# Whole-chunk sample attention with the last-landed tile first, and the mixers' weight loads from SP

## The chip, the cores and the metric

The kernel runs on one core of one Trainium2 chip. The metric is the time of one execution on the device in microseconds (us); the kernel before took 1676.75 us (median of 3 runs, 1676.6 to 1680.71).

## What is computed

One inference step of a two-layer decoder trunk in float32, for 256 tokens of a new sequence (the prompt) and 64 tokens that continue eight cached sequences (the sample, 8 each).

```python
D_MODEL = 1024; SEQ = 256; DEC_BATCH = 8; DEC_SEQ = 8; PAST_LEN = 2048; PAGE_SIZE = 128; D_FF = 2816
# each layer:
#   x += 0.5 * SwiGLU(RMSNorm(x))
#   x += W_out [HGRN2 | RWKV-7 | MLA](RMSNorm(x) @ W_in)
#   x += 0.5 * SwiGLU(RMSNorm(x))
# one RMSNorm ends the stack
```

MLA is an attention with a low-rank cache: for each cached token a latent of 256 numbers (ckv) and a rotary key of 32 (kpe). The prompt attends to itself. Each sample token attends to its sequence's 2048 cached tokens, which lie in 16 pages of 128 tokens each, found through a page table, and to the new ones. HGRN2 and RWKV-7 are recurrences, done in chunks.

## The kernel before

Activations are kept transposed, 128 features by 320 tokens to a tile. Each dense weight is loaded as float32 ("raw"), cast on ACT into a high part (L422), and DVE takes the difference as a low part (L423); PE does three matmuls a block of 128 x 128: high x high, high x low and low x high. Weights of the ffn stages come from `wf` in transfers of 512 KB, issued by SP; those of the mixers from `wm` in transfers of 256 KB, issued by ACT (`fetch_raw`, L363), where a load is placed after the cast before last (`issue_after`, which orders instructions for the scheduler). Four raw buffers are used in turn.

The stages follow each other: ffn, mixer 0, ffn, ffn, mixer 1, ffn. A mixer begins with dense work alone: `mla_in` and `mla_q`, which make the queries. Then `weave` (L513) interleaves generators: the input projections, the two recurrences (rw, hg), the prompt's attention (`prompt`), the sample's attention (`sample`) and the part of the output projection that is ready (`w_out`). A generator yields the time at which its next step will be ready in the planner's own count of PE time (`self.pe`), and `weave` takes the first one that is. The order so written is then scheduled by the framework. At the end `mix_out` (L603) does the rest of the output projection.

The sample works on four pairs of sequences p, each in four chunks ch of 512 cached tokens. `scores(p, ch)` needs four ct tiles (keys, 96 x 768, for one sequence and two pages each), `values(p, ch)` four cn tiles (128 x 512). Each tile is loaded by two DMAs, one a page, whose page number SP reads from the table into a register before it; so a chunk of either kind takes eight gathers on SP. There are five buffers for ct tiles and five for cn tiles. For the values the scores are transposed on PE (L290), copied by DVE to PT, and multiplied. The pairs run one behind the other: values of pair p and scores of pair p + 1 alternate.

When a chunk may be planned is set by `ready` (L843): it charges 1.05 us of planned time for each page load, 4 at a time (half a chunk), and lets loads start no earlier than the end of the half-chunk three back. This is where the planner learns that buffers and SP's time are limited:

```python
f[0] = max(f[0], f[1][f[2] - 3] if f[2] > 2 else 0.0) + n * (PACE[1] if f[2] < PACE[0] else 1.05)
```

Of the kernel before, what the change touches and what calls it, by code (L numbers as in the profile page):

```python
# [26 lines left out]
RANK = 256  # L27
# [4 lines left out]
NPOOL = 160  # L32
PAGE = 128
NPAGE = 16
# [2 lines left out]

FBLK, MBLK = 8, 4
LEVELS = [32, 16, 8, 4, 2, 1]
PACE = (0, 1.05)  # L40
ORDER_A = lambda fill, sample: (sample, fill)
ORDER_B = lambda prompt, sample: (sample, prompt)

# [213 lines left out]
class Kern:  # L257
    def __init__(self, ctx, tc, ap):
        self.ctx, self.tc, self.nc, self.ap = ctx, tc, tc.nc, ap
        P = lambda name, bufs, **k: ctx.enter_context(tc.tile_pool(name=name, bufs=bufs, **k))  # L260
        self.cp = P("cp", 1)
        self.xp = P("xp", 1)
        self.wp = P("wp", 1)
        self.ps = P("ps", 1, space=bass.MemoryType.PSUM)
        self.n = 0
        self.gat, self.early, self.casts = [], [], []
        self.pe = 0.0

        self.st = {"wf": [FBLK, 0, None, None], "wm": [MBLK, 0, self.wp, None]}
        self.cur = "wf"  # L270
# [92 lines left out]
    def fetch_raw(self, i):  # L363
        n, _, pool, _ = self.st[self.cur]
        raw = self.t(pool, [128, n * 128], "raw", bufs=RAW)
        if self.cur == "wf":
            return raw, self.nc.sync.dma_start(raw, self.ap["wf"][i])

        with self.tc.issue_after(self.casts[-2]) if len(self.casts) > 1 else ExitStack():
            return raw, self.nc.scalar.dma_start(raw, self.ap["wm"][i])  # L370

    def fetch(self):
        raw, ins = self.fetch_raw(len(self.early))
# [176 lines left out]
    def mixer(self, l):  # L550
        nc, tc = self.nc, self.tc
        self.l = l
        self.pe, self.ready, self.ended, self.ev = 0.0, {}, [], {}
        xh, xl = self.tiles(self.xh, KD), self.tiles(self.xl, KD)
        pool = lambda name: tc.tile_pool(name=f"{name}{l}", bufs=1)
        with pool("mx") as self.mp, pool("ms") as self.sp, tc.tile_pool(name=f"mk{l}", bufs=1, side="right") as self.tb:
            self.idx_setup(l)
            with pool("mq") as self.ta:
                self.mla_in(xh, xl)
                self.mla_q()  # L560
            sample = self.sample()
            with pool("mr") as self.ta:
                rin = self.rw_in(xh, xl)
                for _ in range(17):
                    next(rin)
                rw = [self.together(*[self.chain(self.rw(hp), self.rw_out(hp)) for hp in range(2)])]
                fill, rws = self.chain(rin, self.hg_in(xh, xl), self.outs()), self.rw_split()
                self.urgent = [*rw, rws]
                self.weave([*rw, *ORDER_A(fill, sample), rws], [*rw, fill, rws])
            with pool("mh") as self.ta, pool("mb") as self.tb:  # L570
                hg, prompt, w_out = [self.together(*[self.hg(hp) for hp in range(2)])], self.prompt(), self.w_out()
                self.urgent = [*hg, prompt]
                order = [*hg, *ORDER_B(prompt, sample), w_out]
                self.weave(order, order)

    def outs(self):

# [56 lines left out]
    def mla_in(self, xh, xl):  # L634
        nc, l = self.nc, self.l
        self.mark(f"mla_in{l}")
        cs = self.a([128, T], "cs")
        nc.sync.dma_start(cs, self.ap["cs"])
        self.wukt = self.a([64, NH, 3 * KR], "wukt")
        nc.sync.dma_start(self.wukt.rearrange("p a b -> p (a b)"), self.ap["wukt"][l])  # L640
        self.qh = self.a([128, 3, T], "qh", dt=F32R)
        self.ql = self.a([128, 3, T], "ql", dt=F32R)
        accq = self.a([128, T], "accq")
        acck = self.a([128, T], "acck")
        self.cT = self.m([128, 2, T], "cT")
        first = [self.bank()[:, :T] for _ in range(2)]
        self.dense_pair(first, KD, xh, xl)
        first.append(self.bank("pr")[:, :T])
        self.dense(first[2], KD, xh, xl)
        self.norm_close()  # L650
        for j in range(6):
            if j < 3:
                ps = first[j]
            else:
                ps = self.bank(("pd", "pr")[j % 2])[:, :T]
                self.dense(ps, KD, xh, xl)
            if j == 4:
                pq = self.bank("pa")[:, :T]
                self.mm(pq, self.c("ones"), accq, start=True, stop=True)
                rq = self.rstd_from(pq, self.ta, "rq", 1.0 / 384)  # L660
                self.csq = self.a([128, T], "csq")
                nc.vector.tensor_tensor(out=self.csq, in0=cs, in1=rq, op=ALU.mult)
            if j < 3:
                qa = self.a([128, T], "qa")
                nc.vector.tensor_tensor(out=qa, in0=ps, in1=self.rstd, op=ALU.mult)
                self.sumsq(qa, accq, j == 0)
                self.split_scaled(qa, self.v(l, "gq", j), self.qh[:, j, :], self.ql[:, j, :])
            elif j == 3:
                csr = self.a([128, T], "qa")
                nc.vector.tensor_tensor(out=csr, in0=cs, in1=self.rstd, op=ALU.mult)  # L670

                t1 = self.a([128, T], "rt1")
                nc.vector.tensor_tensor(out=t1[64:], in0=ps[64:], in1=csr[64:], op=ALU.mult)
                for r in (64, 96):
                    nc.vector.tensor_tensor(out=self.kpe[r:r + 32], in0=t1[64:96], in1=t1[96:128], op=ALU.add)
                nc.sync.dma_start(self.ap["o_kpe"][l], self.kpe[64:96, :])
            else:
                nc.vector.tensor_tensor(out=self.cT[:, j - 4, :], in0=ps, in1=self.rstd, op=ALU.mult)
                self.sumsq(self.cT[:, j - 4, :], acck, j == 4)
        self.acck = acck  # L680
# [140 lines left out]
    def sample(self):  # L821
        nc, l = self.nc, self.l
# [12 lines left out]

        def ready(name, n):
            f = feed[name]
            f[0] = max(f[0], f[1][f[2] - 3] if f[2] > 2 else 0.0) + n * (PACE[1] if f[2] < PACE[0] else 1.05)
            f[2] += 1
            return 0, f[0] + 2.2  # L840

# [8 lines left out]

        def scores(p, ch):
            ps = self.bank("pa")
            for hf in range(2):
                yield ready("ct", 4)
                self.mark(f"sample{l}")
                cts = []
                for si in range(2):
                    ct = self.s([KR, 2, 3 * PAGE], "ct", 5)
                    i0 = (2 * p + si) * NPAGE + ch * 4 + hf * 2
                    for pg, r in enumerate(pages(i0, 2)):  # L860
                        self.gat.append(nc.sync.dma_start(ct[:, pg, :], ctp[bass.ds(r + l * NPOOL, 1)].rearrange("a p c -> p (a c)")))
                    cts.append(ct)
                for kt in range(3):
                    for si in range(2):
                        self.mm(ps[64 * si:64 * si + 64, hf * 256:hf * 256 + 256], qlat[:KR, kt, 2 * p + si],
                                cts[si][:, :, kt * PAGE:kt * PAGE + PAGE], start=kt == 0, stop=kt == 2)
                feed["ct"][1].append(self.pe)
            S[p, ch] = self.s([128, 512], "S", 5)
            if ch == 0:
                mx[p] = self.s([128, 8], "smx", 2)  # L870
# [19 lines left out]
            nc.scalar.activation(S[p, ch], S[p, ch], AF.Exp, bias=m[:, 5:6], scale=MLA_SCALE, accum_out=m[:, ch:ch + 1])  # L890

        def values(p, ch, po):
            r0 = ready("cn", 4)
            cns_ = []
            rs = []
            for si in range(2):
                i = (2 * p + si) * NPAGE + ch * 4
                rs.append(pages(i, 4))
            for hf in range(2):
                for si in range(2):  # L900
                    cn = self.s([128, 2, RANK], "cn", 5)
                    for pg in range(2):
                        r = rs[si][hf * 2 + pg]
                        self.gat.append(nc.sync.dma_start(cn[:, pg, :], self.ap["cn"][l, bass.ds(r, 1)].rearrange("a p c -> p (a c)")))
# [8 lines left out]
            PT = self.s([128, 512], "PT", 2)  # L913
            nc.vector.tensor_copy(PT, pt)  # L914
            yield 0, max(self.pe + 1.2, r0[1])
            for hf in range(2):
                self.mark(f"sample{l}")
                for pg in (2 * hf, 2 * hf + 1):
                    for si in range(2):
                        self.mm(po[64 * si:64 * si + 64, :RANK], PT[:, pg * 128 + 64 * si:pg * 128 + 64 * si + 64],  # L920
                                cns_[2 * hf + si][:, pg % 2, :], start=ch == 0 and pg == 0, stop=False)
                feed["cn"][1].append(self.pe)
                if hf == 0:
                    yield ready("cn", 4)

        for ch in range(4):
            yield from scores(0, ch)
# [552 lines left out]
def build(ctx, tc, ap):  # L1480
    K = Kern(ctx, tc, ap)
    for l in range(L + 1):
# [13 lines left out]
            if l < L:  # L1496
                K.ffn(fp, (l, "gm"), False)
        if l < L:
            K.cur, K.casts = "wm", []
            K.mixer(l)  # L1500


# [19 lines left out]
```

## Time and profile before

| | us |
|---|---|
| median of 3 runs | 1676.75 |
| profiled execution | 1678.2 |
| its span | 1676.4 |
| PE busy | 1627.8 (97%) |
| DVE busy | 958.7 (57%) |
| ACT busy | 716.8 (43%) |

The span is the time from the first to the last instruction that the profiler saw. A busy share over the whole span is a mean over stages with different limits: here the ffn stages from 14 to 250, 597 to 1080 and 1426 to 1667 us and the mixers between them. SP does no arithmetic; its time is seen in the starts of the DMA instructions that it issues. "ct<-in_ct x8" is eight gathers that follow each other without another kind between them, with the start of the first and the stretch to the end of the last.

### The profile page before, as it was taken

What the parts mean: (1) busy time and instruction counts of PE and PEld (TensorE: products, weight loads), DVE (VectorE), ACT (ScalarE), POOL (GpSimd) and SP (SyncE); (2) the same over time, 40 slices, a digit from 0 to 9 for tenths busy, and PEclk for the clock granted to TensorE, in tenths of its full rate; (3) what the DMA queues carried; (4) which work ended last, traced back from release to release, by engine and by line L of the source; (5) the groups of instructions that cost most, each with busy time, mean ns of one, the idle gap of its engine ahead of it and who ended that gap; (6) DMA issues with size and microseconds to landing.
All of it is one profiled execution on the core that took longest, in us unless ns stands there. A gap on an engine that the chain in (4) does not pass through costs nothing. (4 is left out here: it accounts for less than half of the span.)

```text
span 1676.4 us, 33385 instructions
## 1 busy us (share of the span) xinstructions
PE 1627.8 (97%) x13174; PEld 1448.2 (86%) x13174; DVE 958.7 (57%) x1599; ACT 716.8 (43%) x1209; POOL 78.3 (5%) x112
## 2 busy tenths in 40 slices
PE   8999999999999899999999999999999998999998
PEld 7999998777557599999999999987765666999998
DVE  7555447844456575554465554478344665655543
ACT  6444334543353354443344443346242543544433
POOL 0000000200031000000000000002000300000000
PEclk9999999999999999999999999999999998999999
DMA  8555526556573454555445555456457545345542
GB/s 268 151 151 149 149 81 175 173 150 178 177 229 112 150 171 149 151 151 151 151 145 149 149 151 150 115 161 185 118 172 217 160 135 180 112 147 147 150 151 93
DMA packets 130908, 260.05 MB, mean 155 GB/s; under 512 B 17264, under 2 KB 75952, under 8 KB 130624
## 3 DMA queue, kind: packets, MB, share of 16 engines
q1 hardware_dynamic: 111584, 223.58, 44.7%
q10 hardware_dynamic: 19136, 34.28, 6.9%
q8 instruction: 104, 1.70, 0.4%
q0 software_dynamic: 32, 0.07, 0.1%
q14 instruction: 52, 0.43, 0.1%
HBM read 253.39 MB, written 4.47 MB: 154 GB/s over the span
## 5 line engine op out<-in xcount | busy, mean ns | idle before, releaser
L423 DVE TENSOR_TENSOR w<-raw,w 128x1024 fp32r<-128x1024 f32 (+1 forms) x392 | 410.0, 1047 | 325.9 <-ACT w L422 319.8
L422 ACT CAST w<-raw 128x1024 fp32r<-128x1024 f32 (+1 forms) x392 | 354.9, 909 | 437.4 <-PE pd L286 190.3
L286 PE MATMUL pd<-xh,w 128*128 128x320 f32 x1792 | 427.6, 317 | 14.4 <-ACT w L422 10.6
L286 PEld LDWEIGHTS pd<-xh,w 128*128 128x128 f32 x1792 | 307.0, 190 | 30.6 <-ACT w L422 14.9
L286 PE MATMUL pd<-xl,w 128*128 128x320 f32 x896 | 282.0, 316 | 0.0
L286 PE MATMUL pr<-xh,w 128*128 128x320 f32 x1056 | 241.7, 311 | 4.4 <-ACT w L422 4.0
L286 PE MATMUL pa<-xh,w 128*128 128x320 f32 x896 | 201.7, 309 | 0.0
L286 PEld LDWEIGHTS pr<-xh,w 128*128 128x128 f32 x1056 | 178.3, 188 | 6.6 <-ACT w L422 5.3
L286 PEld LDWEIGHTS pd<-xl,w 128*128 128x128 f32 x896 | 170.5, 190 | 5.6 <-issue 4.6
L286 PE MATMUL pr<-xl,w 128*128 128x320 f32 x528 | 162.5, 309 | 0.0
L286 PE MATMUL pd<-hh,w 128*128 128x320 f32 x704 | 158.2, 309 | 0.0
L286 PE MATMUL pr<-hh,w 128*128 128x320 f32 x704 | 158.2, 309 | 0.0
L286 PEld LDWEIGHTS pa<-xh,w 128*128 128x128 f32 x896 | 151.0, 188 | 0.0
L286 PE MATMUL pa<-xl,w 128*128 128x320 f32 x448 | 137.6, 309 | 0.0
L286 PE MATMUL pa<-ct,qlat 96*64 96x256 f32 x768 | 119.9, 393 | 0.8 <-ACT w L422 0.4
L286 PEld LDWEIGHTS pd<-hh,w 128*128 128x128 f32 x704 | 118.4, 188 | 0.0
L286 PEld LDWEIGHTS pr<-hh,w 128*128 128x128 f32 x704 | 118.4, 188 | 0.0
L286 PE MATMUL pd<-hl,w 128*128 128x320 f32 x352 | 108.8, 309 | 0.0
L286 PE MATMUL pr<-hl,w 128*128 128x320 f32 x352 | 108.8, 309 | 0.0
L286 PEld LDWEIGHTS pr<-xl,w 128*128 128x128 f32 x528 | 99.1, 188 | 0.4
L470 ACT ACTIVATE fa<-fa 128x320 f32<-128x320 f32 x88 | 41.5, 472 | 134.0 <-DVE fa L469 133.9
L286 PEld LDWEIGHTS pa<-ct,qlat 96*64 96x64 f32 x768 | 59.9, 138 | 38.3 <-issue 14.2
(381 smaller groups left out, 2010.4 us busy)
## 6 DMA issues: line engine op xcount, KB each, us to landing
raw<-in_wf SPq DMA_DIRECT2D x264, 512.0 KB, 3.6
ct<-in_ct SPq DMA_DIRECT2D x256, 144.0 KB, 2.8
raw<-in_wm ACTq DMA_DIRECT2D x128, 256.0 KB, 3.1
cn<-in_cn SPq DMA_DIRECT2D x256, 128.0 KB, 2.4
xT<-in_x SPq DMA_DIRECT2D x4, 320.0 KB, 6.9
wukt<-in_wukt SPq DMA_DIRECT2D x2, 576.0 KB, 6.3
S<-in_rws SPq DMA_DIRECT2D x4, 256.0 KB, 3.5
o_rws<-S SPq DMA_DIRECT2D x4, 256.0 KB, 2.7
```

The lines of the kernel that those rows point to most:

```text
L286: self.last = self.nc.tensor.matmul(out, w, x, start=start, stop=stop)
L422: self.cast = nc.scalar.copy(h, src).ins
L423: nc.vector.tensor_tensor(out=lo, in0=src, in1=h.bitcast(F32), op=ALU.subtract)
L470: nc.scalar.activation(a, a, AF.Silu)
```

## The change

Three things are edited. (1) The wm loads outside the weave (for `mla_in`, `mla_q` and `mix_out`) are issued by SP without waiting for a cast; inside the weave they stay on ACT, after the cast third from last. The loads of cs and wukt, the first pair's ct gathers and, behind a mixer, the wf loads are ordered after certain wm loads. (2) A scores chunk and a values chunk are each one step, which uses its four tiles from the last to the first; the last pair's odd values chunks use ct buffers. (3) `ready` lets a chunk's loads start when the chunk before it has been used; it charges 8 loads at once. `PACE` becomes the number 1.05.

```diff
-        if self.cur == "wf":
-            return raw, self.nc.sync.dma_start(raw, self.ap["wf"][i])
-
-        with self.tc.issue_after(self.casts[-2]) if len(self.casts) > 1 else ExitStack():
-            return raw, self.nc.scalar.dma_start(raw, self.ap["wm"][i])
+        if self.woven:
+
+            with self.tc.issue_after(self.casts[-3]):
+                return raw, self.nc.scalar.dma_start(raw, self.ap["wm"][i])
+
+        with self.tc.issue_after(self.raws[-1]) if self.cur == "wf" and self.raws else ExitStack():
+            ins = self.nc.sync.dma_start(raw, self.ap[self.cur][i])
+        if self.cur == "wm":
+            self.raws.append(ins.ins)
+        return raw, ins
...
         first = [self.bank()[:, :T] for _ in range(2)]
         self.dense_pair(first, KD, xh, xl)
+        with self.tc.issue_after(self.raws[-1]):
+            nc.sync.dma_start(cs, self.ap["cs"])
         first.append(self.bank("pr")[:, :T])
         self.dense(first[2], KD, xh, xl)
+        with self.tc.issue_after(self.raws[-1]):
+            nc.sync.dma_start(self.wukt.rearrange("p a b -> p (a b)"), self.ap["wukt"][l])
...
         def ready(name, n):
             f = feed[name]
-            f[0] = max(f[0], f[1][f[2] - 3] if f[2] > 2 else 0.0) + n * (PACE[1] if f[2] < PACE[0] else 1.05)
+            f[0] = max(f[0], f[1][f[2] - 1] if f[2] else 0.0) + n * PACE
...
         def scores(p, ch):
             ps = self.bank("pa")
+            yield ready("ct", 8)
...
-                yield ready("ct", 4)
...
+                    n = 6 + 2 * (4 * ch + 2 * hf + si)
+                    with self.tc.issue_after(self.raws[n]) if p == 0 and n < len(self.raws) else ExitStack():
...
+            for hf in (1, 0):
                 for kt in range(3):
-                    for si in range(2):
+                    for si in (1, 0):
...
         def values(p, ch, po):
-            r0 = ready("cn", 4)
+            r0 = ready("cn", 8)
...
-                    cn = self.s([128, 2, RANK], "cn", 5)
+
+                    cn = self.s([128, 2, RANK], "ct" if p == 3 and ch % 2 else "cn", 5)
...
-            for hf in range(2):
-                self.mark(f"sample{l}")
-                for pg in (2 * hf, 2 * hf + 1):
-                    for si in range(2):
...
-                feed["cn"][1].append(self.pe)
-                if hf == 0:
-                    yield ready("cn", 4)
+            self.mark(f"sample{l}")
+            for pg in (3, 2, 1, 0):
+                for si in (1, 0):
...
+            feed["cn"][1].append(self.pe)
```

How the instructions move is shown at three places. First PE near the end of mixer 0 before: the program's pieces of scores (pa<-ct), hg (pr), transposes (L290) and w_out (pd<-xh).

```order
L286 MATMUL pa_5785<-ct_5794,qlat_2430 64x256
L286 MATMUL pa_5785<-ct_5860,qlat_2430 64x256
L286 MATMUL pr_6483<-EX_1031_6342 64x64 x8
L286 MATMUL pr_6550<-AT_976_5939,EX_1027_6307 64x64 x4
...
L286 MATMUL pr_6667<-EX_1027_6307,cf_70 128x320
...
L286 MATMUL pa_5785<-ct_5868,qlat_2430 64x256
L290 MATMUL pa_5915<-cf_70,S_5230 128x128 x4
L286 MATMUL pd_6517<-xh_5718,w_1043_6421 128x320
...
L286 MATMUL pr_6684<-EX_1031_6342,cf_70 128x320
L286 MATMUL pa_5968<-ct_5969,qlat_2430 64x256
```

Here one scores chunk is cut in two, with hg between its halves, and w_out stands between two chunks. Second the same end of the mixer on PE as it is now, from the last prompt matmuls (pd_6523) on.

```order
L286 MATMUL pv_4944<-cn_5233,PT_5293 64x256
...
L286 MATMUL pd_6523<-pPT_6520,V_5440 64x128 x2
L286 MATMUL pv_4944<-cn_5398,PT_5493 64x256
...
L286 MATMUL pa_5569<-ct_5594,qlat_2430 64x256
...
L290 MATMUL pa_5653<-cf_70,Sn_4843 64x128
...
L290 MATMUL pa_5728<-cf_70,S_5047 128x128 x4
L286 MATMUL pv_5695<-cn_5724,PT_5733 64x256
...
L286 MATMUL pa_5838<-ct_5911,qlat_2430 64x256
```

The chunks follow each other to the end of the sample with nothing between them but the steps of the sample itself: nine values chunks and five scores chunks, in either layer. Third SP at the start of mixer 0, where TENSOR_LOAD reads page numbers and ISA puts one in an address; before:

```order
L367 DMA raw_2352<-in_wf 128x1024
L367 DMA raw_2382<-in_wf 128x1024
L638 DMA cs_2435<-in_cs 128x320
L640 DMA wukt_2437<-in_wukt 64x2304
L845 TENSOR_LOAD pti_2428
L861 ISA
L861 DMA ct_3108<-in_ct 96x384
```

and now, with the first wm loads on the same engine:

```order
L372 DMA raw_2382<-in_wf 128x1024
L372 DMA raw_2598<-in_wm 128x512
L372 DMA raw_2624<-in_wm 128x512
L654 DMA cs_2435<-in_cs 128x320
L658 DMA wukt_2436<-in_wukt 64x2304
L854 TENSOR_LOAD pti_2428
L873 ISA
L873 DMA ct_3108<-in_ct 96x384
...
L873 DMA ct_3116<-in_ct 96x384
L372 DMA raw_2642<-in_wm 128x512
L372 DMA raw_2670<-in_wm 128x512
```

Earlier blocks than raw_2598 stand further up, among the ffn's loads; the later ones stand between the gathers.

## Rows read from the trace of the kernel before

**Rows 1.** The page, parts 1 and 2: busy us, and tenths in 40 slices.

```profile
PE 1627.8 (97%) x13174; PEld 1448.2 (86%) x13174; DVE 958.7 (57%) x1599; ACT 716.8 (43%) x1209; POOL 78.3 (5%) x112
...
PE   8999999999999899999999999999999998999998
```

**Rows 2.** Stretches: us, busy (x) of PE, PEld, DVE, ACT, POOL, PEclk, DMA share, GB/s.

```profile
250.00:597.00 347.00, 331.82 (x3320) 242.81 (x3319) 205.57 (x411) 149.28 (x324) 36.10 (x50) 0.99 0.57 171
1080.00:1426.00 346.00, 328.18 (x3288) 239.88 (x3287) 204.45 (x407) 145.81 (x319) 36.12 (x50) 0.97 0.57 168
1401.00:1411.00 10.00, 8.95 (x54) 7.07 (x53) 2.87 (x8) 1.84 (x6) 0.00 (x0) 0.50 0.15 29
```

**Rows 3.** Waits of PE, 1080 to 1110 us, then 250 to 290: total, times, longest.

```profile
PE pr L286 <- ACT w L422: 1.8, 1, 1.8
PE pd L286 <- ACT w L422: 0.8, 1, 0.8
...
PE pr L286 <- ACT w L422: 1.4, 1, 1.4
PE pd L286 <- ACT w L422: 0.6, 1, 0.6
```

**Rows 4.** Timeline from 250 us, ACT, then SP: start, us, what, [idle before].

```profile
251.53 0.33 ACTq L370 DMA_DIRECT2D raw<-in_wm  x1
257.27 0.62 ACT L422 CAST w<-raw 128x512 fp32r<-128x512 f32 x1 [2.75 <-DMA raw<-in_wm]
...
250.38 0.33 SPq L638 DMA_DIRECT2D cs<-in_cs  x1
...
252.52 8.62 SPq L861 DMA_DIRECT2D ct<-in_ct  x10
```

**Rows 5.** Waits of PE, 540 to 600 us, then 1370 to 1430.

```profile
PE pa L290 <- ACT S L890: 1.9, 1, 1.9
PE pv L286 <- DMA cn<-in_cn: 1.2, 2, 0.6
PE pr L286 <- ACT w L422: 0.8, 2, 0.5
...
PE pv L286 <- DMA cn<-in_cn: 3.1, 2, 2.6
PE pd L286 <- ACT w L422: 1.7, 1, 1.7
PE pa L290 <- DVE PT L954: 0.6, 1, 0.6
```

**Rows 6.** Timeline of SP, 480 to 503 us, and at 1365 us.

```profile
487.47 5.41 SPq L861 DMA_DIRECT2D ct<-in_ct  x8
493.48 4.55 SPq L904 DMA_DIRECT2D cn<-in_cn  x8
498.73 4.04 SPq L861 DMA_DIRECT2D ct<-in_ct  x6
...
1365.74 28.07 SPq L904 DMA_DIRECT2D cn<-in_cn  x31
```

**Rows 7.** Tile cn (min/median/max ns), and median us to landing, 493 to 501.

```profile
L904 SPq DMA_DIRECT2D cn<-in_cn x256: 332/333/1759, 333.6 to 1395.0; - x128
...
cn<-in_cn SPq DMA_DIRECT2D x8, 128.0 KB, 2.1
```

**Rows 8.** The chain that ended last, near the end of mixer 1: start, us, what.

```profile
1360.95 0.59 PE pa L290 x4
1363.83 1.45 PE pa L286 x12
1365.28 1.73 PE pv L286 x16
1385.05 1.01 PE pv L286 x6
```

**Rows 9.** The same chain, where mix_out's weights are waited for.

```profile
1412.15 6.91 DMA raw<-in_wm
```

More of the change, by code (lines that the diff above doesn't have):

```diff
@@ L39 @@
 LEVELS = [32, 16, 8, 4, 2, 1]
-PACE = (0, 1.05)
+PACE = 1.05
 ORDER_A = lambda fill, sample: (sample, fill)
@@ L265, in __init__ @@
         self.n = 0
-        self.gat, self.early, self.casts = [], [], []
+        self.gat, self.early, self.casts, self.raws, self.woven = [], [], [], [], False
         self.pe = 0.0
@@ L561, in mixer @@
             sample = self.sample()
+            self.woven = True
             with pool("mr") as self.ta:
@@ L574, in mixer @@
                 self.weave(order, order)
+            self.woven = False
     def outs(self):
@@ L637, in mla_in @@
         cs = self.a([128, T], "cs")
-        nc.sync.dma_start(cs, self.ap["cs"])
         self.wukt = self.a([64, NH, 3 * KR], "wukt")
-        nc.sync.dma_start(self.wukt.rearrange("p a b -> p (a b)"), self.ap["wukt"][l])
         self.qh = self.a([128, 3, T], "qh", dt=F32R)
@@ L852, in scores @@
             ps = self.bank("pa")
+            yield ready("ct", 8)
+            self.mark(f"sample{l}")
+            cts = []
             for hf in range(2):
-                yield ready("ct", 4)
-                self.mark(f"sample{l}")
-                cts = []
                 for si in range(2):
                     ct = self.s([KR, 2, 3 * PAGE], "ct", 5)
-                    i0 = (2 * p + si) * NPAGE + ch * 4 + hf * 2
-                    for pg, r in enumerate(pages(i0, 2)):
-                        self.gat.append(nc.sync.dma_start(ct[:, pg, :], ctp[bass.ds(r + l * NPOOL, 1)].rearrange("a p c -> p (a c)")))
+                    rs = pages((2 * p + si) * NPAGE + ch * 4 + hf * 2, 2)
+                    n = 6 + 2 * (4 * ch + 2 * hf + si)
+                    with self.tc.issue_after(self.raws[n]) if p == 0 and n < len(self.raws) else ExitStack():
+                        for pg, r in enumerate(rs):
+                            self.gat.append(nc.sync.dma_start(ct[:, pg, :], ctp[bass.ds(r + l * NPOOL, 1)].rearrange("a p c -> p (a c)")))
                     cts.append(ct)
+            for hf in (1, 0):
                 for kt in range(3):
-                    for si in range(2):
+                    for si in (1, 0):
                         self.mm(ps[64 * si:64 * si + 64, hf * 256:hf * 256 + 256], qlat[:KR, kt, 2 * p + si],
-                                cts[si][:, :, kt * PAGE:kt * PAGE + PAGE], start=kt == 0, stop=kt == 2)
-                feed["ct"][1].append(self.pe)
+                                cts[2 * hf + si][:, :, kt * PAGE:kt * PAGE + PAGE], start=kt == 0, stop=kt == 2)
+            feed["ct"][1].append(self.pe)
             S[p, ch] = self.s([128, 512], "S", 5)
@@ L892, in values @@
         def values(p, ch, po):
-            r0 = ready("cn", 4)
+            r0 = ready("cn", 8)
             cns_ = []
-            rs = []
-            for si in range(2):
-                i = (2 * p + si) * NPAGE + ch * 4
-                rs.append(pages(i, 4))
+            rs = [pages((2 * p + si) * NPAGE + ch * 4, 4) for si in range(2)]
             for hf in range(2):
                 for si in range(2):
-                    cn = self.s([128, 2, RANK], "cn", 5)
+                    cn = self.s([128, 2, RANK], "ct" if p == 3 and ch % 2 else "cn", 5)
                     for pg in range(2):
@@ L915, in values @@
             yield 0, max(self.pe + 1.2, r0[1])
-            for hf in range(2):
-                self.mark(f"sample{l}")
-                for pg in (2 * hf, 2 * hf + 1):
-                    for si in range(2):
-                        self.mm(po[64 * si:64 * si + 64, :RANK], PT[:, pg * 128 + 64 * si:pg * 128 + 64 * si + 64],
-                                cns_[2 * hf + si][:, pg % 2, :], start=ch == 0 and pg == 0, stop=False)
-                feed["cn"][1].append(self.pe)
-                if hf == 0:
-                    yield ready("cn", 4)
+            self.mark(f"sample{l}")
+            for pg in (3, 2, 1, 0):
+                for si in (1, 0):
+                    self.mm(po[64 * si:64 * si + 64, :RANK], PT[:, pg * 128 + 64 * si:pg * 128 + 64 * si + 64],
+                            cns_[2 * (pg // 2) + si][:, pg % 2, :], start=ch == 0 and pg == 3, stop=False)
+            feed["cn"][1].append(self.pe)
         for ch in range(4):
@@ L1498, in build @@
         if l < L:
-            K.cur, K.casts = "wm", []
+            K.cur, K.casts, K.raws = "wm", [], []
             K.mixer(l)
```

## The prediction

> **What bounds the kernel now.** I read four views, in this order. The page first: TensorE (PE) is busy 97% of the span, and its digits fall below 9 only at the first slice and at the ends of the two mixers [rows 1]. The table by stage then says where PE has room at all: ffn stretches have none, mixer 0 (250 to 597 us) lacks 347.00 - 331.82 = 15.2 us and mixer 1 (1080 to 1426 us) 346.00 - 328.18 = 17.8 us [rows 2]. So the kernel is bound by PE, and a change gains by what it takes from these 33 us and loses by every stretch in which PE runs out of work. Third, the waits of PE in the two stretches that the change touches: at the mixers' starts PE waits for casts on ACT, 1.4 + 0.6 us in layer 0 and 1.8 + 0.8 us in layer 1 [rows 3]; ACT in turn waits for the weight block ("DMA raw<-in_wm", 2.75 us), while SP puts the cs table, wukt and ten page gathers on the queues from 250.38 us on [rows 4]. At the ends PE waits for value pages (cn), weight casts and an exponential: 1.2, 0.8 and 1.9 us in layer 0, 3.1, 1.7 and again 1.9 us in layer 1 [rows 5]. Fourth, SP, the engine that issues all page gathers. Its pace is what my forecast hangs on: eight ct gathers (one scores chunk) begin at 487.47 us, the eight cn gathers (one values chunk) at 493.48, the next ct at 498.73 [rows 6]. Unhindered, a scores chunk costs SP 6.01 us and a values chunk 5.25 us, 11.26 us a pair, though a DMA instruction itself takes only 0.33 us [rows 7]; the rest is the reading of page numbers into registers. The same pair costs PE 2 x 1.45 + 0.59 + 1.73 = 5.2 us [rows 8]. **A pair that stands alone on PE therefore starves it for about 6 us; a pair among other matmuls does not.**
>
> **The change, part by part.**
>
> *Start of a mixer.* The first weight blocks go to SP, ahead of cs, wukt and the gathers; four raw buffers limit them and no longer a cast. In the order of SP two blocks stand before cs now, and blocks stand between the gathers. The waits of rows 3 should go: -2.0 and -2.6. Added: weight issues of about 0.33 us on SP, as ACT's issues of the same transfers take [rows 4], where SP has nothing urgent until the first scores chunk.
>
> *End of a mixer.* mix_out's weights come from SP too, and wf loads stay behind the last of them. In layer 1 a block of mix_out's is waited for 6.91 us in the chain [rows 9]; PE's share of that is the 1.7 us of rows 5, in layer 0 it is 0.8 us. I take both off: -2.5. SP pays again about 0.33 us a block, behind the last gather.
>
> *Whole chunks, last tile first.* A scores chunk is no longer cut into two halves and a values chunk not into two; a chunk's half-array matmuls then run in one piece. In the trace 16 records of a values chunk in one piece take 1.73 us, 0.108 each; pieces of 6 take 1.01 us, 0.36 more than 6 x 0.108 [rows 8]. In the order of PE the unbroken runs of values matmuls fall from 73 to 40 and those of scores from 91 to 78. 46 breaks fewer at 0.11 us (between 0 and 0.36, since some of a piece's start is a wait) are -5; ends 0 and -8.
>
> *The planner's gate.* This is the dear part. Loads of a chunk are now planned to start only when the chunk before it is consumed, not the half-chunk three back. So the planner puts every chunk later. In the order of PE this leaves, at the end of each mixer, a tail: after the last prompt matmuls (pd_6523 in layer 0) come 9 values chunks and 5 scores chunks with no dense, hg or prompt matmul between them. Before, hg, w_out and prompt matmuls stood between most of these chunks. The price, from the end of the values chunk ahead of pd_6505 (its release lets SP go on; five buffers hold one chunk and a quarter, so two of eight gathers are out already): SP issues 3/4 x 5.25 + 8 x 5.25 + 5 x 6.01 = 76.0 us, the last page lands 2.1 us later [rows 7], and the last chunk's matmuls take 1.73: 79.8 us. PE has in it 9 x (1.73 + 0.59) + 5 x 2.9 = 35.4 us, with about 2 us of prompt matmuls and 2.6 us of the closing steps of two pairs: 40.0. **Stall 39.8 us a mixer, +80 in all.** Bounds: if the register work hides between issues, a chunk costs only the spans in rows 6 without the pauses between groups (5.41 and 4.55), which gives 70.7 - 40.0 = 31 us; if PE's clock falls and PE itself paces part of it, 48 us (below). I take the paces with pauses, as measured from start to start. A check of it on the kernel before: its last 31 cn gathers took 28.07 us where each chunk waits for the buffers of the one before [rows 6], 7.2 us a chunk, so SP is not faster than I assume.
>
> The Trainium skill (DMA: Bandwidth & Descriptors, "Issuing engines are not separate DMA queues") says that the time on the sequencer to initiate a DMA is usually small relative to the DMA itself. The rows speak against it for these gathers: 0.66 to 0.75 us of SP per gather against 2.1 us to landing for one, with several in flight. By that rule the tail would be bounded by transfers, and the first rival below would hold.
>
> *What the tail swallows.* The waits of rows 5 for cn (1.2 and 3.1) and for S (1.9 twice) lie in that stretch: -8.1. The 0.6 us for PT [rows 5], in the closing steps of the last pair, stay.
>
> *Chunks early in the weave.* The order has about four places per mixer where a chunk follows its like with less PE work than its loads need, 0.4 to 5.6 us short each, 9 together. SP is idle before most of them, so I take 4 a mixer: +8 (bounds 0 and 20).
>
> *Clock.* After the waits of 1393 to 1400 us the granted clock was 0.50 from 1401 to 1411 us, with PE busy 8.95 us [rows 2], so about 4.5 us of PE work were lost. A tail in which PE works half the time should bring more of this: inside the tail it is covered, since a pair at half clock is 10.4 us against 11.26; behind it layer 0 pays about 4.5 us once, layer 1 what it pays already. +5 (bounds 0 and 20).
>
> *PACE* becomes one number; the value used was 1.05 already. Nothing.
>
> **Sum.** +79.6 - 4.6 - 2.5 - 5 - 8.1 + 8 + 5 = +72.4. On the profiled execution (1678.2 us, span 1676.4) that is 1750.6; the median of the runs is 1676.75, 1.45 lower, so I say **1749 us**, 4% slower.
>
> **The rivals.**
>
> 1. *SP is not the bound (the other side).* If gathers can follow each other at the price of the DMA instruction, 16 x 0.33 = 5.3 us a pair, PE (5.2 us) is just fed. The point that decides is a pair at 5.3 us on SP. Then only gains remain: -4.6 - 2.5 - 5 - 8.1 + 4 (some early chunks) = -16, so 1660. Against it: rows 6 show twice that time with nothing waited for. Chance 5%.
> 2. *PE at half clock becomes the pace-maker.* In the tail every values chunk has transposes, a copy on DVE and matmuls in a row, with nothing to fill. At half clock nine values chunks and five scores chunks are 2 x 35.4 = 70.8 us, with 0.6 us of waiting for each copy (as for PT in rows 5) and the doubled rest 85 to 88 us; it outlasts the 79.8, so +8 a mixer, and behind each tail another 5 us are lost: +21 over my sum, 1770. For it: rows 2 show 0.50 after a much shorter lull. Against: a busy half may keep the clock. Chance 20%.
> 3. *The tail is shorter.* SP could be a few chunks ahead when it begins, if the planner's gate binds less on the chip than in its plan. Half the stall gives 1749 - 40 = 1709. Against: five buffers hold a chunk and a quarter, which allows 5 us of lead, not 20. Chance 8%.
> 4. *The change does not do what it says at the start*: cs, wukt and the first gathers stand behind only two weight blocks, so later blocks may still arrive late. Then the 4.6 us stay: 1754. Chance 15% beside the others; it lies in the range.
>
> **How the numbers follow.** My forecast, with or without rival 4, has 65%, rival 2 20%, rival 3 8%, rival 1 5%; 2% are left for no change by accident of signs. The bounds of the tail (31 and 48 us a mixer, -17 and +16) and of early chunks and clock (-13 and +27) do not fall together; the forecast's own range is 1725 to 1775. To leave out no more than 2 in 10, with rival 2 and part of rival 3: 1712 to 1782. A measurement here tells 0.3%, 5 us, from no change. Faster by more: 0.05 (rival 1). Within: 0.02. Slower: 0.93.
>
> **What would show it.** In the profile after, the table by stage should have both mixers longer by 35 to 40 us with the same PE work, the ffn stretches unchanged. In the last 75 us of each mixer SP should issue ct x8 and cn x8 back to back at 6.0 and 5.25 us, and PE should wait there for ct and cn pages, about 40 us in all. PE's waits for casts in the first 30 us of a mixer should be under 1 us, and the landing of in_wm at the ends no longer in the chain. The granted clock should be low for part of each tail. I am wrong if SP is seen idle in the tail, if a gather there takes well under 0.6 us of SP, or if other matmuls fill the tail after all.

## The result and the profile after

The changed kernel takes 1768.59 us (median of 4 runs, 1766.71 to 1776.68) against 1676.67 us beside it: 1.0559 times as long, 95% interval 1.0539 to 1.0579. The forecast was 1749 us, with a range of 1712 to 1782. The profiled execution took 1766.71 us with a span of 1764.9, 88.5 us more than the span before.

The page of the changed kernel, parts 1 and 2, answers to [rows 1].

```profile
PE 1667.0 (94%) x13174; PEld 1482.6 (84%) x13174; DVE 954.0 (54%) x1599; ACT 721.2 (41%) x1209; POOL 80.5 (5%) x112
...
PE   8999999998997799999999999999999967999998
...
PEclk9999999999898799999999999999989977999999
```

PE has the same 13174 instructions, is busy 39 us longer and has dips to 6 and 7 tenths where the mixers end. The row of the clock (PEclk, the share of TensorE's full clock that was granted) falls in the same slices and, to 8 tenths, a little ahead of them.

The table by stretch for the changed kernel (us, busy and count of PE, PEld, DVE, ACT, POOL, PEclk, DMA share, GB/s) divides each mixer into its start (to the second norm after `mla_in`), the weave up to the last values chunk that has other work beside it, the tail, and what follows to the next norm.

```profile
252.30:278.90 26.60, 24.85 (x163) 23.19 (x162) 22.79 (x44) 13.74 (x27) 0.00 (x0) 1.00 0.75 207
278.90:535.50 256.60, 242.10 (x2655) 178.26 (x2654) 147.12 (x296) 111.02 (x241) 36.79 (x50) 0.96 0.45 129
535.50:618.00 82.50, 59.27 (x355) 38.30 (x351) 17.64 (x40) 13.44 (x34) 0.00 (x0) 0.75 0.66 190
618.00:654.20 36.20, 34.10 (x236) 31.52 (x236) 26.29 (x51) 18.38 (x36) 0.00 (x0) 0.95 0.56 175
1121.10:1149.40 28.30, 25.14 (x163) 23.21 (x163) 22.92 (x44) 13.69 (x27) 0.00 (x0) 1.00 0.79 192
1149.40:1406.40 257.00, 247.13 (x2645) 181.12 (x2644) 145.18 (x290) 110.75 (x236) 37.60 (x50) 0.95 0.44 128
1406.40:1495.60 89.20, 63.60 (x362) 39.91 (x363) 19.61 (x45) 16.75 (x42) 0.00 (x0) 0.71 0.61 178
1495.60:1528.70 33.10, 31.66 (x231) 29.82 (x232) 24.66 (x48) 16.90 (x34) 0.00 (x0) 1.00 0.41 136
```

The same boundaries in the kernel before:

```profile
252.30:279.30 27.00, 24.62 (x156) 22.20 (x155) 22.43 (x42) 13.78 (x26) 0.00 (x0) 1.00 0.76 208
279.30:610.10 330.80, 318.01 (x3240) 231.41 (x3239) 193.40 (x389) 143.75 (x312) 36.10 (x50) 0.98 0.55 166
1077.90:1105.50 27.60, 24.66 (x157) 22.20 (x156) 22.45 (x42) 13.71 (x26) 0.00 (x0) 1.00 0.75 202
1105.50:1439.40 333.90, 319.02 (x3237) 232.79 (x3236) 192.76 (x386) 142.39 (x309) 36.12 (x50) 0.97 0.54 161
```

A mixer's weave, tail and end took 330.8 and 333.9 us and take 375.3 and 379.3: all the loss is there. The tails have 355 and 362 of PE's instructions in 82.5 and 89.2 us, at a granted clock of 0.75 and 0.71, with PE idle for 23.2 and 25.6 us.

What PE waits for in the tail of mixer 0 (total, times, longest), and behind the "..." what it waits for at the start of mixer 1:

```profile
PE pa L286 <- DMA ct<-in_ct: 11.3, 4, 4.0
PE pv L286 <- DMA ct<-in_cn: 3.7, 1, 3.7
PE pv L286 <- DVE PT L926: 3.1, 4, 0.8
...
PE pr L286 <- DVE w L428: 1.7, 1, 1.7
PE pd L286 <- ACT w L427: 0.7, 1, 0.7
```

The longest waits are for pages, as forecast; "ct<-in_cn" is a values chunk in ct buffers. They are 15.0 us in this tail and 17.4 in that of mixer 1. At the start of mixer 1 the waits of [rows 3] are not gone: the longest is now for the low part of a later block, which DVE makes (L428).

SP's timeline in the tail of mixer 0 answers to [rows 6].

```profile
549.68 6.00 SPq L873 DMA_DIRECT2D ct<-in_ct  x8
556.23 5.03 SPq L916 DMA_DIRECT2D cn<-in_cn  x8
561.96 5.63 SPq L873 DMA_DIRECT2D ct<-in_ct  x8
568.13 4.53 SPq L916 DMA_DIRECT2D cn<-in_cn  x8
573.38 5.98 SPq L873 DMA_DIRECT2D ct<-in_ct  x8
579.91 4.53 SPq L916 DMA_DIRECT2D cn<-in_cn  x8
585.15 5.91 SPq L873 DMA_DIRECT2D ct<-in_ct  x8
```

SP hardly rests: scores and values chunks follow each other, 12.28, 11.42 and 11.77 us from pair to pair, and in the whole tail of 82.5 us SP waits for a buffer for 4.3 us.

### The profile page after: what moved, and what is told of

The parts are those of the page before. It is cut to its first block, busy times and chain, and to the rows that moved or that the text cites. A ratio compares the mean times of both kernels' runs of the same rounds, so it can differ in the third digit from the quotient of the medians.

```text
span 1764.9 us, 33399 instructions
## 1 busy us (share of the span) xinstructions
PE 1667.0 (94%) x13174; PEld 1482.6 (84%) x13174; DVE 954.0 (54%) x1599; ACT 721.2 (41%) x1209; POOL 80.5 (5%) x112
## 4 chain that ended last, share of the span: by engine, by line
PE 87%; DMA 4%; SPq 3%; DVE 2%; ACT 2%; issue 1%; DVEq 0%; ACTq 0%
PE pd L286 33%; PE pr L286 30%; PE pa L286 20%; PE pv L286 4%; DMA ct<-in_ct 2%; PE pa L290 1%; SPq L873 1%; SPq L854 1%; DMA raw<-in_wm 1%; SPq L916 1%; DVE w L428 0%; DMA xT<-in_x 0%; DMA cn<-in_cn 0%; PE pd L290 0%; DMA raw<-in_wf 0%
## 5 line engine op out<-in xcount | busy, mean ns | idle before, releaser
L428 DVE TENSOR_TENSOR w<-raw,w 128x1024 fp32r<-128x1024 f32 (+1 forms) x392 | 410.8, 1050 | 322.6 <-ACT w L427 311.9
L286 PE MATMUL pd<-xh,w 128*128 128x320 f32 x1792 | 421.6, 315 | 10.6 <-ACT w L427 8.5
L286 PEld LDWEIGHTS pd<-xh,w 128*128 128x128 f32 x1792 | 303.4, 189 | 30.4 <-issue 10.9
L286 PE MATMUL pa<-ct,qlat 96*64 96x256 f32 x768 | 132.4, 463 | 39.1 <-DMA ct<-in_ct 35.8
L286 PEld LDWEIGHTS pa<-ct,qlat 96*64 96x64 f32 x768 | 79.0, 164 | 74.6 <-issue 42.8
```

The costliest lines, as they stand in the source:

```text
L286: self.last = self.nc.tensor.matmul(out, w, x, start=start, stop=stop)
L428: nc.vector.tensor_tensor(out=lo, in0=src, in1=h.bitcast(F32), op=ALU.subtract)
```

## The experiments

Three theories stood at the outset. Theory 1: the planner's gate alone makes the tail. Theory 2: the whole chunks do. Theory 3: the weight loads on SP do. For the tail itself a second question was whether SP, PE at half clock, or the transfers pace it.

**The gate alone**, in the kernel before:

```diff
-f[0] = max(f[0], f[1][f[2] - 3] if f[2] > 2 else 0.0) + ...
+f[0] = max(f[0], f[1][f[2] - 1] if f[2] > 0 else 0.0) + ...
```

> The kernel before with one edit: a half-chunk's loads are planned from the end of the half-chunk before it, not of the one three back. Halves, page order and weight loads stay as before. Theory 1 (the planner's gate makes the tail): the last 12 to 14 chunks of each mixer stand alone on PE, PE waits some 40 us there in each, and the time is 1740 to 1775. Theory 2 (that a chunk must have all four tiles at once is the cost): no tail, 1670 to 1690. Theory 3 (the weight loads on SP are the cost): 1677, as before.

Measured: 1774.34 us, ratio 1.058 (1.0551 to 1.061), as much as the whole change. The stretches from the tenth last values chunk to the last, in this kernel:

```profile
526.60:616.70 90.10, 61.80 (x380) 31.76 (x381) 14.98 (x34) 11.64 (x30) 0.00 (x0) 0.94 0.64 185
1397.20:1490.80 93.60, 67.56 (x366) 31.86 (x367) 14.23 (x32) 11.97 (x29) 0.00 (x0) 0.85 0.61 180
```

The tail is there without whole chunks and without the loads, and slightly longer. SP's pairs of chunks come there at the same pace, 11.3 to 12.8 us (mixer 0). PE is idle 28.3 us in the first tail (90.10 - 61.80) and the clock is 0.94: that loss is no matter of the clock.

**The change without the gate:**

```diff
-f[0] = max(f[0], f[1][f[2] - 1] if f[2] else 0.0) + n * PACE
+f[0] = f[0] + n * PACE
```

> The changed kernel with the gate taken out of the planner (a chunk's loads are planned 8 x 1.05 us after those of the chunk before, whenever that is used). Theory 1: the chunks stand among other work again and the time falls by 85 to 100 us, to 1665 to 1685; SP then waits for buffers and no longer PE for pages. Theory 2: 1740 or more, since chunks are still whole. Theory 3: 1740 or more, since the loads are still on SP.

Measured: 1690.82 us, ratio 1.0082 (1.0047 to 1.0116). Some 80 of the 92 us go with the gate. Theory 1 holds for these, but the rest is no gain: 14 us over the kernel before, where I expected between a loss of 8 and a gain of 12. The edit leaves the planner no limit at all, not even the one that the kernel before has (three half-chunks back).

**Whole chunks without the gate**, in the kernel before: the new `scores` and `values`, with the last odd values chunks in ct buffers, and again no limit in the planner.

> The kernel before with only whole chunks, used from the last tile to the first, and no gate in the planner; weight loads as before. Theory 1: no tail, and the fewer breaks between half-array matmuls give 5 to 7 us: 1665 to 1675. Theory 2: PE waits for the fourth tile of each chunk, 1700 or more.

Measured: 1699.65 us, ratio 1.0117 (1.0086 to 1.0148). A miss: this costs 21 us. In mixer 0 PE waits for pages:

```profile
PE pa L286 <- DMA ct<-in_ct: 7.9, 5, 3.6
PE pv L286 <- DMA ct<-in_cn: 2.7, 1, 2.7
PE pv L286 <- DMA cn<-in_cn: 2.1, 1, 2.1
```

That is 12.7 us in this mixer and 26.0 in both, where the kernel before has 4.7 in both. So theory 2 may be true for a fifth of the loss: a whole chunk starts when its eighth gather has landed, with buffers for one chunk and a quarter. But two things differ from the kernel before, whole chunks and a planner without its limit; no run has one without the other, so what each of them costs is not shown.

**The loads alone**, in the kernel before: `fetch_raw`, `mla_in` and the orders of the change, nothing in the sample but the place of the first ct gathers.

> The kernel before with only the first part of the change: wm loads outside the weave on SP, cs and wukt and the first pair's ct gathers behind them. My sum: -4.6 at the starts and -2.5 at the ends, so 1668 to 1672. The profile after shows the start as long as before (26.6 and 28.3 us between the two norm matmuls against 27.0 and 27.6), so the rival is that the waits only change their place: 1674 to 1679. Theory 3: 1740 or more.

Measured: 1676.06 us (10 runs), ratio 0.9979 (0.9959 to 1.0). The rival is right: the waits change place. At the mixers' starts PE now waits 1.2 and 2.4 us for a low part from DVE (L428), where it waited 2.0 and 2.6 us for casts [rows 3]. Theory 3 is out.

**PE given idle work in the tail:**

```diff
+            hold(p == 3 or (p, ch) == (2, 3), ps)   # scores
+            hold(p > 1, pt)                         # values
+        def hold(on, ps):
+            for _ in range(4 if on else 0):
+                nc.tensor.matmul(ps[:, :T], idt, self.cf[:, 128:128 + T], start=True, stop=True)
```

> The changed kernel with idle work for PE: four matmuls of 128 x 320 (some 2.1 us at full clock) ahead of each of the 13 chunks that follow the first of the tail, into the bank that the chunk overwrites; 52 a mixer, 28 us of PE work that the kernel does not need. If SP paces the tail, the tail stays at 78 to 84 us although PE has 28 us more to do, and the time is 1755 to 1775; if in addition the granted clock returns to 1.00 there, what the clock cost (over the 79.8 us that I worked out) is seen as the difference to 82.5 and 87.5 us. If PE at half clock paces it, the extra work counts double and the time is 1820 or more.

Measured: 1780.76 us, ratio 1.061 (1.0582 to 1.0637), a little over the range that I gave. The tails:

```profile
544.90:630.00 85.10, 75.20 (x443) 48.93 (x445) 13.60 (x34) 11.85 (x29) 0.00 (x0) 0.90 0.60 177
1421.50:1512.80 91.30, 77.25 (x459) 53.88 (x460) 19.81 (x47) 18.57 (x45) 0.17 (x1) 0.91 0.56 169
```

The idle matmuls keep PE busy for 30.1 and 30.8 us of the tails, and the tails grow by 2.6 and 2.1 us only (by 5.6 and 6.8 us if they are counted from SP's first scores gather in them); the clock is 0.90 and 0.91 instead of 0.75 and 0.71. So neither PE's work nor its clock sets the tail's length: of the idle 23.2 us only 9.9 are left, but SP is not sooner done. It is even held a little, by buffers that PE releases later: 9.2 us in mixer 0's tail, before 4.3. Its profiled span is 17.2 us longer than the change's; 4.7 of these are the tails, and 9.6 and 3.9 lie ahead of them (292.8 against 283.2 us in mixer 0, 289.2 against 285.3 in mixer 1), where nothing was meant to change and the clock was 0.94 and 0.95 against 0.96. Why is not shown; the two profiled executions took 1783.94 and 1766.71 us, where the medians are 1780.76 and 1768.59. In the next run the same stretch of mixer 0 takes 290.5 us.

**Fewer page reads on SP:** the page numbers of a scores chunk four at a time.

```diff
+            rss = [pages((2 * p + si) * NPAGE + ch * 4, 4) for si in range(2)]
...
-                    rs = pages((2 * p + si) * NPAGE + ch * 4 + hf * 2, 2)
+                    rs = rss[si][2 * hf:2 * hf + 2]
```

> The changed kernel with SP reading the page numbers of a scores chunk four at a time, as a values chunk does: two reads a chunk and not four. If SP paces the tail, a scores chunk costs SP 5.25 us and not 6.01, and mixer 0, where the tail has the same 13 chunks in the same order, ends 3.5 to 4.5 us earlier; the whole is 1758 to 1764. If PE at half clock or the transfers pace it, mixer 0's tail stays within 1 us of 82.5 and the time at 1768.

Measured: 1775.85 us, ratio 1.0584 (1.053 to 1.0637): the whole shows no gain. SP in the tail of mixer 0:

```profile
570.49 4.40 SPq L874 DMA_DIRECT2D ct<-in_ct  x8
575.42 4.52 SPq L917 DMA_DIRECT2D cn<-in_cn  x8
580.48 4.39 SPq L874 DMA_DIRECT2D ct<-in_ct  x8
585.40 4.91 SPq L917 DMA_DIRECT2D cn<-in_cn  x8
590.83 4.71 SPq L874 DMA_DIRECT2D ct<-in_ct  x8
```

The pair takes 9.99 and 10.35 us instead of 11.4 to 12.3, and the tail 80.2 us instead of 82.5, less than the 3.5 us I gave as the least. The tail begins with 6.0 us before SP's first scores gather, where the change has 2.9; from that gather on it takes 74.2 us instead of 79.6, which is 5.4 less. But the stretch ahead of it took 290.5 us at a clock of 0.94, and in mixer 1 the order moved and one values chunk kept SP for 18.41 us. As a test of the total it is inconclusive; in mixer 0 the pace followed SP's reads.

**More page reads on SP:** each number by a read of its own, in the change and in the kernel before.

```diff
-    self.pti[0:1, i:i + n], ...)[1]
+    [... self.pti[0:1, j:j + 1], ...)[1][0] for j in range(i, i + n)]
```

> The changed kernel with SP reading every page number by itself: 4 reads more in a scores chunk, 6 more in a values chunk, 0.38 us each by the difference between the two kinds of chunk (6.01 - 5.25 us for two reads). If SP paces the tails, 5 x 1.5 + 9 x 2.3 = 28 us are added to each, and the time is 1815 to 1835. If PE at half clock or the transfers pace them, 1765 to 1780.

Measured: 1799.33 us, ratio 1.0741 (1.0696 to 1.0786). The tails take 97.0 and 100.6 us:

```profile
538.90:635.90 97.00, 60.13 (x347) 38.01 (x349) 15.01 (x37) 12.10 (x31) 0.00 (x0) 0.72 0.54 157
1423.40:1524.00 100.60, 61.88 (x352) 38.78 (x353) 15.03 (x38) 11.29 (x30) 0.00 (x0) 0.73 0.53 156
```

14.5 and 11.4 us more, with about the same clock and the same work of PE. The direction is that of SP's pace; the size is half of what I expected, because ten more reads cost a pair about 2.1 us (13.6 and 14.0 us from pair to pair) and not 3.8. That is 0.21 us a read; my 0.38 came from the difference of two unlike chunks. SP's trace has the reads themselves (TENSOR_LOAD), here in mixer 0's tail of the change, with fewer reads and with more (count, min/median/max ns, first and last start):

```profile
L854 SPq TENSOR_LOAD <-pti x36: 296/468/481, 537.8 to 610.0; - x36
L854 SPq TENSOR_LOAD <-pti x26: 295/298/303, 548.3 to 612.9; - x26
L854 SPq TENSOR_LOAD <-pti x105: 261/269/279, 539.3 to 629.5; - x105
```

A read of two numbers takes 0.47 us, one of four 0.30 and one of one 0.27. So the change reads for 20 x 0.47 + 16 x 0.30 = 14.2 us in this tail; 26 x 0.30 = 7.8 is 6.4 less (5.4 less from the first scores gather on), 105 x 0.27 = 28.4 is 14.2 more (the tail 14.5). The length of mixer 0's tail follows the time that SP spends on reads.

> The kernel before with the same extra reads on SP. In its weave a pair of chunks comes every 14 to 18 us, and SP needs 15.1 us for one now: where chunks stand among other work the extra is mostly hidden, and only the last 5 to 10 chunks of each mixer pay, 2 us each. 1690 to 1715, a third of what the change pays for the same edit. Rival (that SP's time counts everywhere alike): 1735 or more.

Measured: 1739.73 us, ratio 1.0364 (1.0325 to 1.0402): outside my range, twice the loss of the change for the same edit, and what the rival gave. The edit adds 320 reads; at 0.21 us they are 67 us, and 61 were lost. I had taken a pair to come every 14 to 18 us in the kernel before. Its SP shows that in the middle of mixer 0's weave it is less:

```profile
446.68 5.00 SPq L861 DMA_DIRECT2D ct<-in_ct  x7
452.22 4.90 SPq L904 DMA_DIRECT2D cn<-in_cn  x8
457.83 6.37 SPq L861 DMA_DIRECT2D ct<-in_ct  x8
464.75 4.54 SPq L904 DMA_DIRECT2D cn<-in_cn  x8
470.00 5.63 SPq L861 DMA_DIRECT2D ct<-in_ct  x8
```

12.2 us for a pair (457.83 to 470.00), nearly without rest. In such stretches the kernel before runs the gathers about as fast as SP can and has PE full beside them (22.92 of 23.96 us): SP is its second bound, close behind PE. It is not so everywhere: of the scores chunk that begins at 498.73, SP issues the eighth gather only 21 us later. I had read SP's pace off one pair and not asked how often pairs come.

**The value pages issued by GpSimd** in the changed kernel.

```diff
-                        self.gat.append(nc.sync.dma_start(cn[:, pg, :], ...
+                        self.gat.append(nc.gpsimd.dma_start(cn[:, pg, :], ...
```

> The changed kernel with the value pages (cn) gathered by GpSimd, which reads their page numbers too; SP issues the key pages alone. If the issuing engine paces the tail, a pair costs SP 6.0 us and the tails shrink by 20 to 30 us each, to 1710 to 1730, unless an issue on GpSimd takes over 0.66 us. If the transfers pace it (their share was 0.66 in the tail), a pair cannot fall under 0.66 x 11.8 = 7.8 us and 1720 is the floor. If PE at half clock paces it, 1768.

Measured: 1751.44 us, ratio 1.044 (1.0416 to 1.0464): a gain of about 20 us over the change (1.0559), a third to a half of what I expected. An issue on GpSimd takes 0.54 us (the median of 224) against 0.33 on SP, and the order of the chunks moved, so the tails can't be set side by side. PE still waits 24.2 us for ct pages and 25.7 us for cn pages in the whole run, together as long as in the change (47.6). The gain agrees with the issuing engine as one bound of the tail, but doesn't show it. Late in mixer 0 GpSimd's gathers wait 2.1, 6.2 and 11.1 us for values matmuls, which release their buffers; so buffers hold the gathers there.

**The last values chunks in ct buffers, alone and with other parts.** The one line of the change that spares SP a wait, in the kernel before:

```diff
-                    cn = self.s([128, 2, RANK], "cn", 5)
+                    cn = self.s([128, 2, RANK], "ct" if p == 3 and ch % 2 else "cn", 5)
```

> The kernel before with only the last pair's odd values chunks in ct buffers. If the gain of the run with loads and ct buffers (1665 against 1675) is the end's waits for cn and the clock behind them (10 us at 0.50 from 1401 us on in layer 1), 1666 to 1672; if it needs the weight loads on SP as well, 1673 to 1677.

Measured: 1663.16 us (5 runs), ratio 0.9909 (0.9879 to 0.994): faster than both kernels, and than I expected.

> The kernel before with the weight loads of the change, and the last pair's odd values chunks in ct buffers; halves and the planner as before. The values chunks at the end then wait less for buffers: PE's waits for cn there (1.2 and 3.1 us) should go, for 1668 to 1675. Rival: SP paces these last chunks, and the time is that of the weight loads alone, 1673 to 1677.

Measured: 1665.37 us, ratio 0.9939 (0.9921 to 0.9956), below my range too. With page numbers read four at a time as well:

> The kernel before with the weight loads of the change, ct buffers for the last odd values chunks, and page numbers of a scores chunk read four at a time. SP has 0.76 us less per scores chunk, mostly where it is hidden: 1660 to 1667. Rival: no difference, 1664 to 1668.

Measured: 1658.55 us, ratio 0.9892 (0.9855 to 0.9928), the fastest kernel here, though its interval overlaps that of the one line alone. What the one line does is seen in its SP (first four) and in the mixers from norm to norm:

```profile
1357.09 4.60 SPq L904 DMA_DIRECT2D cn<-in_cn  x8
1362.23 5.21 SPq L904 DMA_DIRECT2D ct<-in_cn  x8
1367.98 6.12 SPq L904 DMA_DIRECT2D cn<-in_cn  x7
...
1375.64 4.36 SPq L904 DMA_DIRECT2D ct<-in_cn  x7
...
250.00:604.60 354.60, 340.78 (x3410) 254.62 (x3409) 216.15 (x431) 157.28 (x338) 36.12 (x50) 0.99 0.57 171
1072.10:1422.30 350.20, 336.89 (x3391) 254.29 (x3390) 213.69 (x427) 154.74 (x334) 36.14 (x50) 0.99 0.57 169
```

The last four chunks leave SP in 24 us (1357.09 to 1381.0), where 31 of their 32 gathers took 28.07 before [rows 6]; of the waits for cn of [rows 5] 0.3 us are left, and in layer 1 the stretch at half clock behind them [rows 2] has shrunk to 5 us at 0.70. That mixer takes 350.2 us from norm to norm, before 361.5 (1077.9 to 1439.4), and mixer 0 354.6 from 250 us on, before 360.1: together 16.8 of the 17.0 us between the two profiled executions.

## Why the prediction was right, and where its terms were off

The forecast named the place and the cause of the loss, and both held: the planner's gate leaves a tail in which SP paces the chunks. Its price was too low, within the range: the sum was +72.4 us; the span grew by 88.5.

| term | predicted | measured |
|---|---|---|
| two tails, over the 40.0 us of PE work in each | +79.6 | 82.5 + 89.2 - 80.0 = +91.7 |
| starts | -4.6 | 26.6 + 28.3 - 27.0 - 27.6 = +0.3 |
| ends, breaks, swallowed waits, early chunks, clock (the rest) | -2.6 | 88.5 - 91.7 - 0.3 = -3.5 |

*The tail.* Its chunks and SP almost without rest are as forecast, and the gate alone brings it (1.058). It was sized at 79.8 us by one pair of chunks, 11.26 us; in the tails a pair takes 11.65 and 11.88 us on average. SP's timeline places the 2.7 and 9.4 us that the tails are longer. Five pairs are 1.9 us more in mixer 0 and 3.1 in mixer 1, the last three values chunks 1.4 and 2.3 (in mixer 1 one took 7.02 us, waiting for buffers), the stretch behind the last gather 0.4 and 1.6. At the start it is 1.0 less and 2.4 more: in mixer 1 SP waits 3.3 us to issue a store of hg's state, and the gathers stand behind it.

That SP's time beyond the 0.33 us of a DMA instruction "is the reading of page numbers" is true in part: four reads of 0.47 us are 1.9 of the 3.4 us that a scores chunk has beyond its eight DMA instructions. The rest lies between the instructions and in setting addresses.

*What PE does in the tail.* The forecast put about 40 us of waiting for pages there. PE waits for them 15.0 and 17.4 us and is idle 23.2 and 25.6 in all: at the lower clock it is busy 59.27 and 63.60 us with what the sum counts as 40.0. For the length this makes no difference as long as SP paces.

*The starts.* This step failed. "The waits of rows 3 should go": the starts are as long as before, as rival 4 had it, with the loads alone (0.9979) to show it. But rival 4's reason, blocks that arrive late, covers at most 0.7 us (a wait for a cast in layer 1). The longest wait, 1.7 us, ends at 1143.57 us, when DVE has made a low part; ahead of it on DVE stands the reciprocal of a norm:

```profile
1140.82 2.15 DVE L451 RECIPROCAL rq<-rq 128x320 f32<-128x320 f32 x1
1142.89 1.23 DVE L428 TENSOR_TENSOR w<-raw,w 128x512 fp32r<-128x512 f32 x2
```

Layer 0 has the same pair ahead of its wait of 1.1 us, and so have both waits of the loads alone. So the blocks come sooner (ACT waits for one for at most 0.73 us in mixer 1, before for 3.12), and PE then waits for DVE, which the forecast did not look at.

*Whole chunks.* The order's fewer breaks were counted as a gain of 5 us, and the early chunks as a loss of 8. (By its own prices the gain had ends 0 and 46 x 0.36 = 17, not 8.) What PE waits for pages ahead of the tails in the changed kernel, mixer 0, then mixer 1:

```profile
PE pa L286 <- DMA ct<-in_ct: 9.8, 3, 5.4
...
PE pa L286 <- DMA ct<-in_ct: 3.9, 2, 2.2
```

With 1.5 us for cn pages in mixer 0 that is 15.2 us, before 0.4: the early chunks were sized too low by about 7 us. The terms that are left in the last row of the table then come to about -18 together, where -10.6 was forecast; what each of them was, no run shows.

*The clock, and rival 2.* Rival 2 (PE at half clock paces the tail) gave 1770 us, and 1768.6 was measured; but its mechanism is not what happened. The clock did fall to 0.75 and 0.71 in the tails (means: 0.50, its lower level, from 585 to 595 us and 1.00 from 560 to 570), where before it was low for some 10 us [rows 2]. With PE given 30 us more to do the clock rose to 0.90 and the tails stayed nearly as long. What clock there was to lose behind the tails was small: 0.95 and 1.00 after them. A rival's number can come out by terms that have nothing to do with it.

*Rival 1* (SP is no bound) is out by SP's timeline; the time from pair to pair is 11.4 to 12.3 us, not 5.3. The Trainium skill (DMA: Bandwidth & Descriptors, "Issuing engines are not separate DMA queues") says that the time on the sequencer to initiate a DMA is usually small relative to the DMA itself. That does not carry to these gathers: in the tail a gather takes about 0.7 us of SP against 2.1 to 2.2 us to its landing, and with several in flight it is SP's share that adds up. *Rival 3* (a shorter tail) is out too: 82.5 and 89.2 us.

*The signs.* SP's chunks back to back, the low clock in the tails, the ffn stretches as before (466.9 us between the mixers, before 467.8) and no wm landing at the ends in the chain came as stated. The mixers grew by 44.1 and 46.1 us, not 35 to 40; the waits at the starts stayed over 1 us.

## What to carry to other kernels

When a planner interleaves a stream of transfers with compute, ask what each chunk costs on the engine that issues its transfers, not only on the one that computes: where chunks stand alone, the larger of the two sets the pace. A gate that says "start loading when the last one is used" is right for buffers and still a loss if it delays the stream beyond the work that should cover it. Read the end of the overlapped stretch first: a single line that let the last chunks use a second pool of buffers was worth 0.9%, the only part of the change that was seen to pay by itself.

## What was not expected of the hardware

A read of one page number takes SP 0.27 us, of two 0.47 and of four 0.30; they stand in line with the DMA issues (each begins 0.04 us behind one), so single reads cost less than the count of reads suggests, and reading four at a time is the cheapest for a page. Why two take longer than four is not shown. The granted clock was 0.75 and 0.71 over the tails, in which PE was idle for 23.2 and 25.6 us, and 0.90 and 0.91 where idle work filled them. But idle time alone doesn't tell the clock: with the gate alone PE was idle for 28.3 us of mixer 0's tail, in many short waits (29 for pages, none over 2.2 us), and the clock there was 0.94. And of the same code ahead of the tails the time differed by 7 to 9 us between kernels (283.2, 290.5 and 292.8 us) with the clock at 0.96, 0.94 and 0.94, which is as large as several terms of the sum.
